# Forming all MLP weight sums on VectorE, and handing the residual stream between two layers through HBM

## The chip, the cores and the metric

One NeuronCore of a Trainium2 chip runs the whole program. The metric is the device time of one execution in microseconds (us). Inputs and weights lie in HBM; the output is written back to HBM. TensorE is called PE in the views, VectorE DVE, ScalarE ACT, GpSimd POOL, and SyncE SP.

## What is computed

The program carries a residual stream x of 1024 frames by 1024 features through two layers, in float32. Layer 0 mixes frames by a gated linear recurrence, layer 1 by an attention with forget gates (FoX, 8 heads); beside either one runs an attention into 256 fixed memory tokens. Each layer then adds a squared-ReLU MLP:

```
for layer in range(2):
    h = rms_norm(x, norm_mix[layer])
    y_mix, xq = rglru_group(h, ...) if layer == 0 else fox_group(h, ...)
    y_mem = memory_group(xq, mem, norm_mem[layer], w_mem_kv[layer], ...)
    x = x + concatenate([y_mix, y_mem]) @ w_out[layer]
    x = x + square(relu(rms_norm(x, norm_mlp[layer]) @ w_mlp_in[layer])) @ w_mlp_out[layer]
```

## The kernel before

**Products.** Each float32 operand is split into a high part, which TensorE takes in its faster float32 form, and a low part, the remainder; a product is three matmuls (high by high, high by low, low by high). The high part of a weight is a copy on ScalarE (L316), the low part a subtraction (L317, on VectorE, for some entries half of it on GpSimd). Activations are split the same way: L468 and L469 in `split`, L474 and L477 in `split_sb`. SP loads raw weights into four buffers `wr`; the split parts go through a ring of three pairs `wh`, `wl`. The list `plan` fixes in which order the weights come.

**Stream.** x is kept transposed, as 8 blocks of 128 features, in two halves of 512 frames, h=0 and h=1. Between stages it lies in HBM, in `xspill` (`self.xs`). `load_x` (L510) brings one block of 128x512 into one of the `f` tiles; `r` tiles hold split activations.

**MLP.** Each layer's MLP runs in 8 groups of hidden features, and each group as two block products of Strassen's kind (`mlp_z`, then `mlp_out`), with seven products of sums of blocks instead of eight of blocks. One product (L1017) is 24 matmuls of 128x512. The seven weight operands of a block product are a unit: the raw blocks a11, a12, a21, a22 and the sums S1 to S4, which `_wunit` forms in place when it reaches S2 (L355 to L357, in two halves of 512, and L360). Only the first unit of a layer's `w1` forms them on VectorE, the others on GpSimd. Some groups of layer 1 are parked: their first two products run earlier, in other stages, so that their unit begins with S2.

In `mlp_out` the block results c11, c21, c22 and c12 leave PSUM as a copy on ScalarE (L1028) and a sum on VectorE (L1033). In groups 0 to 6 a result is then added in HBM by an accumulating DMA of GpSimd (`send`, L1172). In group 7 of both layers the old x is added on the chip instead: for c11 by GpSimd (L1192) from tiles loaded before, for c21 and c22 by an accumulating DMA from HBM into the tile (L1195), for c12 by starting from a loaded tile. Then `sink` stores the block by SP (L1177). In layer 0 `sink` also squares each block on ScalarE (L438), sums the squares (L444, on GpSimd, a few on VectorE) and, for the half h=0, splits it as the input of layer 1's mixer.

**After layer 0.** `kv` projects the memory tokens (L385; its norm's products are L590, the sum of its squares L597 on GpSimd). `norm_fin` turns the sum of squares into the norm factor: four one-column matmuls (L378) add over the partitions. `xq_proj` projects the memory queries of h=0, `fox_proj` queries, keys and values, `fox` is the attention, `outproj` the output projection, run once for the attention's half of the weights (`wout1x`) and once for the memory's (`wout1m`), each in 8 pieces with a weight entry of 512 columns apiece. `weave(a, b, rate)` runs steps of b between steps of a.

The program's text is put into each engine's order by a scheduler at compile time; every engine then works through its own list, with semaphores between them.

## Time and profile before

| | us |
|---|---|
| median of three runs | 2134.29 |
| lowest and highest of the runs | 2131.2 and 2135.48 |
| the profiled execution | 2132.37 |
| its span in the trace | 2130.7 |
| TensorE busy in it | 2071.5 |
| VectorE busy | 1663.3 |
| ScalarE busy | 1141.9 |
| GpSimd busy | 864.0 |

1.7 us of the profiled execution lie outside its span. Layer 0's MLP lies from about 340 to 985 us of the span, layer 1's from about 1530 to the end; the handover between the layers is the stretch from about 930 to 1005 us.

How to read the rows: in a timeline, start, duration, engine, line, operation, output<-input with the tile shape, and a count; in brackets the idle time of the engine before it and what ended it. In a group of instructions: the count, then busy time, the mean in ns, and idle time. In a list of waits: total, times, longest. L12 is line 12 of the kernel.

### The profile page before, as it was taken

Reading aid. Unit: us, or ns where it says so; the run is one execution under the profiler, and the core shown is the slowest. Engines: PE = TensorE matmul, PEld = TensorE weight load, DVE = VectorE, ACT = ScalarE, POOL = GpSimd, SP = SyncE. Lnnn points to the kernel's source line nnn. Section 1 sums busy time; section 2 is a strip of 40 time slices with the busy share of each in tenths; the row PEclk is TensorE's granted clock in tenths of the full one; section 3 lists DMA queues with packets and bytes.
Section 4 is the critical chain, followed back from the end, with each engine's and each line's share of the span. In section 5 each row is a group of like instructions: output and inputs, shape, how many; then the busy total and the mean of one; then the engine's idle time right before and its main releaser. Section 6 shows DMA issues by size and latency. Waiting matters only on the chain. (4 is left out here: it accounts for less than half of the span.)

```text
span 2130.7 us, 30055 instructions
## 1 busy us (share of the span) xinstructions
PE 2071.5 (97%) x10466; PEld 1727.4 (81%) x10466; DVE 1663.3 (78%) x2708; ACT 1141.9 (54%) x2160; POOL 864.0 (41%) x844
## 2 busy tenths in 40 slices
PE   9999999999999999988999999999999999999998
PEld 8898878878778778767998998777777877787786
DVE  7988698877877877887677778776787768868777
ACT  6755655544454454555555646566544554445443
POOL 2222321535535525545342333422054645445444
PEclk8999999999999999989999999999999999999999
DMA  5422452546545635627768446934546675364474
GB/s 180 140 77 93 135 184 94 101 89 128 101 97 119 111 87 119 156 86 199 276 218 290 133 138 214 299 122 129 161 99 139 138 150 101 85 140 94 89 173 119
DMA packets 126392, 298.44 MB, mean 140 GB/s; under 512 B 14176, under 2 KB 16288, under 8 KB 126240
## 3 DMA queue, kind: packets, MB, share of 16 engines
q1 hardware_dynamic: 82464, 208.36, 29.4%
q0 software_dynamic: 43776, 88.17, 23.2%
q8 instruction: 82, 1.34, 0.3%
q14 instruction: 70, 0.57, 0.1%
HBM read 187.32 MB, written 109.15 MB: 139 GB/s over the span
## 5 line engine op out<-in xcount | busy, mean ns | idle before, releaser
L317 DVE TENSOR_TENSOR wl<-wr,wh 128x1024 fp32r<-128x1024 f32 (+2 forms) x362 | 441.2, 1229 | 108.5 <-ACT wh L316 104.1
L1017 PE MATMUL pspt<-r,wh 128*128 128x512 f32 x1536 | 485.1, 396 | 7.2 <-DVE r L477 2.6
L1172 POOL DMA_DIRECT2D xspill<-f x224 | 284.7, 1963 | 287.5 <-DVE f L1033 284.1
L316 ACT ACTIVATE wh<-wr 128x1024 fp32r<-128x1024 f32 (+3 forms) x411 | 306.0, 766 | 141.4 <-PE pss L1017 41.2
L1017 PEld LDWEIGHTS pspt<-r,wh 128*128 128x128 f32 x1536 | 289.0, 188 | 77.9 <-DVE r L477 4.3
L1017 PE MATMUL pss<-r,wh 128*128 128x512 f32 x1024 | 329.6, 400 | 19.8 <-ACT f L1028 8.1
L477 DVE TENSOR_TENSOR r<-f,r 128x512 fp32r<-128x512 f32 x282 | 230.1, 826 | 98.5 <-ACT r L474 39.9
L1017 PE MATMUL pspt<-r,wl 128*128 128x512 f32 x768 | 305.6, 398 | 0.2
L1017 PE MATMUL pspj<-r,wh 128*128 128x512 f32 x832 | 265.8, 399 | 2.1 <-DVE f L1033 1.0
L1017 PEld LDWEIGHTS pss<-r,wh 128*128 128x128 f32 x1024 | 192.6, 189 | 75.9 <-DVE r L477 13.9
L385 PE MATMUL pspj<-wh,r 128*128 128x256 f32 (+1 forms) x1280 | 248.5, 286 | 2.3 <-DVE r L1322 0.8
L474 ACT ACTIVATE r<-f 128x512 fp32r<-128x512 f32 x282 | 173.5, 626 | 106.2 <-DMA xspill<-f 49.0
L1038 ACT ACTIVATE f<-f 128x512 f32<-128x512 f32 x128 | 80.9, 632 | 269.5 <-DVE f L1037 269.4
L385 PEld LDWEIGHTS pspj<-wh,r 128*128 128x128 f32 x1280 | 201.6, 188 | 5.3 <-DVE r L1322 1.0
L1017 PE MATMUL pss<-r,wl 128*128 128x512 f32 x512 | 203.6, 398 | 0.0
L355 POOL TENSOR_TENSOR wr<-wr,wr 128x512 f32<-128x512 f32 x60 | 95.7, 1778 | 249.0 <-DVE wl L317 233.2
L1017 PEld LDWEIGHTS pspj<-r,wh 128*128 128x128 f32 x832 | 156.3, 189 | 39.4 <-DVE r L469 1.5
L385 PE MATMUL pspj<-wl,r 128*128 128x256 f32 (+1 forms) x640 | 181.1, 283 | 0.0
L1017 PEld LDWEIGHTS pspt<-r,wl 128*128 128x128 f32 x768 | 146.0, 190 | 36.9 <-DVE wl L317 2.0
L385 PE MATMUL pspj<-r,wh 128*128 128x512 f32 x488 | 164.1, 411 | 5.3 <-ACT r L474 2.1
L1017 PE MATMUL pspj<-r,wl 128*128 128x512 f32 x416 | 163.4, 397 | 0.6 <-DVE wl L317 0.5
L357 POOL TENSOR_TENSOR wr<-wr,f 128x512 f32<-128x512 f32 x60 | 135.4, 2550 | 17.1 <-issue 17.1
(301 smaller groups left out, 4035.3 us busy)
## 6 DMA issues: line engine op xcount, KB each, us to landing
wr<-in_w_dram SPq DMA_DIRECT2D x136, 512.0 KB, 4.5
xspill<-f POOLq DMA_DIRECT2D x224, 256.0 KB, 7.0
f<-xspill SPq DMA_DIRECT2D x88, 256.0 KB, 4.1
xspill<-f SPq DMA_DIRECT2D x64, 256.0 KB, 3.5
f<-in_xT_dram SPq DMA_DIRECT2D x32, 256.0 KB, 3.5
wr<-in_wkv_dram SPq DMA_DIRECT2D x16, 512.0 KB, 3.6
...
```

The source lines that it names most:

```text
L316: self.wact = self.nc.scalar.activation(hi, raw, AF.Copy)
L317: eng.tensor_tensor(lo, raw, hi.bitcast(F32), ALU.subtract)
L355: G.tensor_tensor(r["a11"][:, d], r["a11"][:, d], r["a21"][:, d], ALU.subtract)
L357: G.tensor_tensor(r["a12"][:, d], r["a12"][:, d], x, ALU.subtract)
L385: self.lastmm = self.nc.tensor.matmul(out, lhsT=a, rhs=b, start=(j == 0), stop=(j == n - 1))
L474: i = self.nc.scalar.activation(hi[:, :n], src, AF.Copy)
L477: self.nc.vector.tensor_tensor(lo[:, :n], src, hi[:, :n].bitcast(F32), ALU.subtract)
L1017: self.lastmm = self.nc.tensor.matmul(ps, lhsT=a, rhs=b, start=(start and c == 0 and j == 0), stop=(c == n - 1 and j == 2), skip_group_che ...
L1038: self.lastsq = self.nc.scalar.activation(f[:, n], f[:, n], AF.Square)
L1172: nc.gpsimd.dma_start(self.xs[2 * q + a, :, b * H:(b + 1) * H], f[:, n], accum_op=ALU.add)
```

## The change

Four things are edited. Every weight unit of the MLP forms its sums on VectorE (`u.dve = True`). Group 7 of layer 0 now does what groups 0 to 6 do: it adds its results in HBM by accumulating DMAs of GpSimd. The next mixer's half h=0 is then loaded from HBM, in the order of blocks 0, 2, 4, 6, 1, 3, 5, 7, by a new `norm_split_back`, which splits each block, squares it on ScalarE and adds over the partitions on TensorE (`sq_pe`: four one-column matmuls for each of the 8 blocks). It is woven one step for one into the memory projection. The squares of h=1 are taken where `norm_split` loads that half, during the fox projection. In layer 1's last group, the c11 add moves from GpSimd to VectorE and behind the second sum. And the entries of `wout1m` and `wout1x` hold two pieces each, 1024 columns wide.

```diff
@@ -463,9 +463,11 @@
                                       start=(m == 0 and t == 0), stop=(m == 7), skip_group_check=True)
             self.F.put(sq)
 
-    def split(self, xt, g, n=H):
+    def split(self, xt, g, n=H, behind=None):
         hi, lo = self.R.get(), self.R.get()
         self.last_hi = self.nc.scalar.activation(hi[:, :n], xt, AF.Copy, scale=g)
+        if behind is not None:
+            self.after(self.last_hi, behind)
         self.nc.vector.scalar_tensor_tensor(lo[:, :n], xt, g, hi[:, :n].bitcast(F32), ALU.mult, ALU.subtract)
         return hi, lo
 
@@ -517,6 +519,15 @@
             if stats:
                 self.sqacc(k, h, x[:, :H])
             xs.append(self.split(x[:, :H], self.pc(g, k)))
+            self.F.put(x)
+            yield
+
+    def norm_split_back(self, h, g, src):
+        xs = self.xg[h] = [None] * 8
+        for j, k in enumerate((0, 2, 4, 6, 1, 3, 5, 7)):
+            x = self.load_x(k, h, src)
+            xs[k] = self.split(x[:, :H], self.pc(g, k), behind=self.wact)
+            self.sq_pe(j, h, x[:, :H], self.last_hi)
             self.F.put(x)
             yield
 
@@ -888,12 +899,15 @@
 
     def outproj(self, h, ks, src, dst, gain, last, banks=("pj",)):
         nc = self.nc
+        per = 8 // len(ks)
         for m in range(8):
             x = self.load_x(m, h, src)
-            wh, wl = self.wnext()
+            if m % per == 0:
+                wh, wl = self.wnext()
             ps = self.psum(banks[m % len(banks)])
             terms = []
             for i, k in enumerate(ks):
+                i += m % per * len(ks)
                 c = slice(i * P, (i + 1) * P)
                 terms += self.t3(wh[:, c], wl[:, c], *(self.ymix[h][k] if k < 4 else self.ymem[h][k - 4]))
             yield from self.mmq(ps, terms, 6)
@@ -1004,8 +1018,9 @@
             self.plan_unit("w1", 8 * l + g, Unit.ALL[1:2])
         for g in range(8):
             u = self.plan_unit("w1", 8 * l + g, Unit.ALL[2:] if g in parked + wait else Unit.ALL)
-            u.dve = g == 0
-            self.plan_unit("w2", 8 * l + g)
+            u.dve = True
+            u = self.plan_unit("w2", 8 * l + g)
+            u.dve = True
 
     def product(self, banks, parts, start, done=None):
         w = self.wnext()
@@ -1152,10 +1167,9 @@
 
     def mlp_out(self, l, g, mid):
         nc = self.nc
-        V, G = nc.vector, nc.gpsimd
+        V = nc.vector
         n = slice(0, H)
         hp = self.hp
-        seen = set()
 
         def run(banks, key, start, done, ahead=None):
             if ahead is not None:
@@ -1172,14 +1186,10 @@
             nc.gpsimd.dma_start(self.xs[2 * q + a, :, b * H:(b + 1) * H], f[:, n], accum_op=ALU.add)
             self.F.put(f)
 
+        last = l == 1 and g == 7
+
         def sink(f, q, a, b):
-            x, dm = f[:, n], 2 * q + a
-            nc.sync.dma_start((self.out if l else self.xs)[dm, :, b * H:(b + 1) * H], x)
-            if l == 0:
-                self.sqacc(1 if b in seen else 0, b, x, V if b == 0 and a == 1 else None)
-                seen.add(b)
-                if b == 0:
-                    self.xg[0][dm] = self.split(x, self.pc("gmix1", dm))
+            nc.sync.dma_start(self.out[2 * q + a, :, b * H:(b + 1) * H], f[:, n])
             self.F.put(f)
 
         def keep(a, b):
@@ -1187,21 +1197,21 @@
 
             def first(q, ps):
                 self.copies(dst)(q, ps)
-                if g == 7 and a == b == 0:
-                    f = self.acc.pop(0)
-                    G.tensor_tensor(dst[q][:, n], dst[q][:, n], f[:, n], ALU.add)
-                    self.F.put(f)
-                elif g == 7:
+                if last and (a or b):
                     nc.gpsimd.dma_start(dst[q][:, n], self.xs[2 * q + a, :, b * H:(b + 1) * H], accum_op=ALU.add)
 
             def then(q, ps):
                 self.plus(dst[q], ps)
-                (sink if g == 7 else send)(dst[q], q, a, b)
+                if last and not (a or b):
+                    f = self.acc.pop(0)
+                    V.tensor_tensor(dst[q][:, n], dst[q][:, n], f[:, n], ALU.add)
+                    self.F.put(f)
+                (sink if last else send)(dst[q], q, a, b)
 
             return first, then
 
         def end(q, ps):
-            if g == 7:
+            if last:
                 self.plus(acc[q], ps)
                 sink(acc[q], q, 0, 1)
             else:
@@ -1217,7 +1227,7 @@
         mid()
         yield from run(A, "t2", False, c21[0], "t1")
         C = [self.psum(k) for k in more]
-        acc = [self.load_x(2 * q, 1, self.xs) for q in range(4)] if g == 7 else None
+        acc = [self.load_x(2 * q, 1, self.xs) for q in range(4)] if last else None
         yield from run(C, "t3", True, c22[0], "t4")
         yield from run(A, "t1", False, c22[1], "b22")
         yield from run(C, "t4", False, c21[1])
@@ -1236,7 +1246,7 @@
         def hook7(key):
             if key in ("t2", "b22") and nxt is not None:
                 advance(nxt)
-            if key == "t1":
+            if key == "t1" and l:
                 self.acc = [self.load_x(2 * q, 0, self.xs) for q in range(4)]
 
         for p in wait:
@@ -1252,7 +1262,6 @@
                 self.F.put(*self.rsb)
                 if l == 0:
                     self.pool_parts = TUNE["pb0"]
-                    self.xg[0] = [None] * 8
             drain(self.mlp_out(l, g, lambda: self.mlp_back(g + 1)))
 
 
@@ -1531,17 +1540,17 @@
         self.plan_mv("wxqb")
         self.plan_fox(0)
         self.plan_fox(1)
-        self.plan += [self.ent("wout1m", m, 512, 1) for m in range(8)]
+        self.plan += [self.ent("wout1m", m, 1024, 1) for m in range(4)]
         self.plan_mv("wxqb")
         self.plan_fox(0)
         self.plan_fox(1)
-        self.plan += [self.ent("wout1x", m, 512, 1) for m in range(8)]
-        self.plan += [self.ent("wout1m", m, 512, 1) for m in range(8)]
+        self.plan += [self.ent("wout1x", m, 1024, 1) for m in range(4)]
+        self.plan += [self.ent("wout1m", m, 1024, 1) for m in range(4)]
         for g in TUNE["park"]:
             self.plan_unit("w1", 8 + g, Unit.ALL[:2])
         for g in TUNE["wait"]:
             self.plan_unit("w1", 8 + g, Unit.ALL[:1])
-        self.plan += [self.ent("wout1x", m, 512, 1) for m in range(8)]
+        self.plan += [self.ent("wout1x", m, 1024, 1) for m in range(4)]
         self.plan_mlp(1, TUNE["park"], TUNE["wait"])
 
         self.share()
@@ -1635,19 +1644,21 @@
 
 
         self.fox_setup()
-        advance(kv, 5)
+        advance(kv, 6)
+        weave(kv, self.norm_split_back(0, "gmix1", self.xs), 1.0)
+        self.vst = {}
+        xq = self.xq_proj(0, 1)
+        advance(xq, 4)
         self.norm_fin(0, False, self.lastmm)
-        drain(kv)
-        self.vst = {}
-        drain(self.xq_proj(0, 1))
-        self.norm_fin(1, False)
+        drain(xq)
         xa = self.xattn(0)
         self.pool_parts = TUNE["pb0"]
         weave(self.fox_proj(0, 0), xa, TUNE["fp00"])
         drain(xa)
         fx = self.fox(0)
         opm = self.outproj(0, K_M, self.xs, self.xs, None, False)
-        weave(self.fox_proj(0, 1), self.norm_split(1, "gmix1", self.xs, False), 0.5)
+        weave(self.fox_proj(0, 1), self.norm_split(1, "gmix1", self.xs, True), 0.5)
+        self.norm_fin(1, False)
         self.xg_free(0)
 
         def second():
@@ -1730,6 +1741,8 @@
     kord = [4, 5, 6, 7, 0, 1, 2, 3]
     for nme, w, ks in (("wout0", w0, kord), ("wout1m", w1, kord[0:4]), ("wout1x", w1, kord[4:8])):
         o[nme] = st(C(w[ks].reshape(-1, D)))
+        if len(ks) == 4:
+            o[nme] = C(o[nme].reshape(4, 2, P, 512).transpose(0, 2, 1, 3).reshape(4, P, 1024))
     w1, w2 = [], []
     for l in range(2):
         w = f["w_mlp_in"][l].reshape(4, 2, P, 8, 2, 2, P).transpose(3, 5, 1, 2, 4, 0, 6).reshape(8, 4, P, 1024)

```

The engines' order in the compiled programs, as rows of line, operation, output<-input, shape and the semaphores waited for. In a tile's name, `f_856_8078` is use 856 of the `f` tiles, while the number of `wr`, `wh` and `wl` is a buffer's; `xspill` is x in HBM. First GpSimd at the end of layer 0's last group. Before:

```order
L597 TENSOR_TENSOR f_838_7994<-f_838_7994,f_849_8026 128x512 [waits Activation_49,Pool_49]
L1192 TENSOR_TENSOR f_860_8102<-f_860_8102,f_830_7911 128x512 [waits DMAHW0_49,Activation_49]
L1192 TENSOR_TENSOR f_861_8111<-f_861_8111,f_831_7913 128x512 [waits DMAHW1_49,Activation_49]
L1192 TENSOR_TENSOR f_862_8120<-f_862_8120,f_832_7915 128x512 [waits DMAHW2_49,Activation_49]
L1192 TENSOR_TENSOR f_863_8129<-f_863_8129,f_833_7917 128x512 [waits DMAHW3_49,Activation_49]
L444 TENSOR_TENSOR f_868_8154<-f_868_8154,f_871_8168 128x512 [waits PE_49,Activation_49]
L444 TENSOR_TENSOR f_868_8154<-f_868_8154,f_874_8183 128x512 [waits Activation_49,Pool_49]
L1269 MEMSET f_924_8492 128x128 [waits PE_49]
L1270 AFFINE_SELECT f_924_8492<-f_924_8492 128x128 [waits Pool_49]
L444 TENSOR_TENSOR f_868_8154<-f_868_8154,f_877_8198 128x512 [waits Activation_49]
L1195 DMA f_884_8221<-xspill 128x512 [waits DMASW0_49,Activation_49]
L1195 DMA f_885_8230<-xspill 128x512 [waits DMASW1_49,Activation_49]
```

After:

```order
L608 TENSOR_TENSOR f_834_7970<-f_834_7970,f_845_8002 128x512 [waits Activation_49,Pool_49]
L1186 DMA xspill<-f_856_8078 128x512 [waits DMASW0_49,DVE_49]
L1186 DMA xspill<-f_857_8086 128x512 [waits DMASW1_49,DVE_49]
L1186 DMA xspill<-f_858_8094 128x512 [waits DMASW2_49,DVE_49]
L1186 DMA xspill<-f_859_8102 128x512 [waits DVE_49]
L1186 DMA xspill<-f_876_8213 128x512 [waits DMASW4_49,DVE_49]
L317 TENSOR_TENSOR wl_76<-wr_69,wh_73 128x256 [waits DMAHW4_49,PE_49,Activation_49]
L1186 DMA xspill<-f_877_8221 128x512 [waits DMASW5_49,DVE_49]
L1186 DMA xspill<-f_878_8229 128x512 [waits DMASW6_49,DVE_49]
L317 TENSOR_TENSOR wl_76<-wr_69,wh_73 128x256 [waits PE_49,Activation_49]
L1186 DMA xspill<-f_879_8237 128x512 [waits DMASW7_49,DVE_49]
L1186 DMA xspill<-f_868_8166 128x512 [waits DMASW0_49,DVE_49]
```

The adds of c11 (L1192), the sums of squares (L444) and the accumulating loads (L1195) are gone; the sends (L1186: c11's `f_856` to `f_859`, c22's `f_876` to `f_879`, then c21's from `f_868`) stand there, with the halves of the memory weights' splits (L317) between them.

Next SP's list at the same place, from the last loads of x before the stores. Before:

```order
L510 DMA f_889_8257<-xspill 128x512 [waits DMAHW0_49,DMASW5_49,PE_49]
L510 DMA f_888_8255<-xspill 128x512 [waits DMAHW1_49,DMASW4_49,PE_49]
L510 DMA f_890_8259<-xspill 128x512 [waits DMAHW2_49,DMASW6_49,PE_49]
L510 DMA f_891_8261<-xspill 128x512 [waits DMAHW3_49,DMASW7_49]
L1177 DMA xspill<-f_860_8102 128x512 [waits DMAHW4_49,DVE_49]
L312 DMA wr_69<-in_wkv_dram 128x1024 [waits DMAHW5_49,DVE_49,Pool_49]
L1177 DMA xspill<-f_861_8111 128x512 [waits DMAHW6_49,DVE_49]
L1177 DMA xspill<-f_862_8120 128x512 [waits DMAHW7_49,DVE_49]
L1177 DMA xspill<-f_863_8129 128x512 [waits DMAHW0_49,DVE_49]
L312 DMA wr_71<-in_wkv_dram 128x1024 [waits DMAHW1_49,DVE_49,Pool_49]
```

After, some steps later, among the weights of the query projection (`wxqb`):

```order
L312 DMA wr_69<-in_wxqb_dram 128x1024 [waits DMAHW1_49,DMAHW5_49,DVE_49,Pool_49]
L512 DMA f_899_8542<-xspill 128x512 [waits DMASW1_49,DVE_49,Activation_49]
L312 DMA wr_70<-in_wxqb_dram 128x1024 [waits DMAHW2_49,DVE_49,Pool_49]
L512 DMA f_907_8624<-xspill 128x512 [waits DMASW2_49,DMAHW6_49,DVE_49,Activation_49]
L312 DMA wr_71<-in_wxqb_dram 128x1024 [waits DMAHW3_49,Pool_49]
L512 DMA f_911_8650<-xspill 128x512 [waits DMASW3_49,PE_49]
L512 DMA f_915_8675<-xspill 128x512 [waits DMASW0_49,PE_49]
L512 DMA f_919_8701<-xspill 128x512 [waits DMASW1_49,DMAHW4_49,PE_49,Activation_49]
L312 DMA wr_72<-in_wxqb_dram 128x1024 [waits DMAHW5_49,DVE_49,Pool_49]
L512 DMA f_923_8746<-xspill 128x512 [waits DMASW2_49,PE_49]
```

The stores (L1177) are replaced by loads of x (L512) that wait for an accumulating DMA (DMASW) to have landed; weight loads stand behind them in the list.

Last, VectorE in a group of layer 1 whose unit begins with S2. Before, the sums of that unit are on GpSimd:

```order
L477 TENSOR_TENSOR r_1778_16425<-f_1729_16083,r_1777_16424 128x512 [waits DVE_49]
L317 TENSOR_TENSOR wl_76<-wr_72,wh_73 128x1024 [waits DMAHW4_49,PE_49,Activation_49]
L477 TENSOR_TENSOR r_1780_16429<-f_1730_16097,r_1779_16428 128x512 [waits Activation_49]
L317 TENSOR_TENSOR wl_77<-wr_70,wh_74 128x1024 [waits PE_49,Activation_49]
L1033 TENSOR_TENSOR f_1773_16398<-f_1773_16398,pss_16232 128x512 [waits PE_49]
L1033 TENSOR_TENSOR f_1774_16406<-f_1774_16406,pss_16233 128x512 [waits PE_49]
L317 TENSOR_TENSOR wl_78<-f_1781_16469,wh_75 128x512 [waits Activation_49]
L1033 TENSOR_TENSOR f_1775_16414<-f_1775_16414,pspj_16234 128x512 [waits DMASW6_49,PE_49]
L1033 TENSOR_TENSOR f_1776_16422<-f_1776_16422,pspj_16235 128x512 [waits PE_49]
L317 TENSOR_TENSOR wl_78<-f_1782_16475,wh_75 128x512 [waits Activation_49]
```

After:

```order
L355 TENSOR_TENSOR wr_69<-wr_69,wr_71 128x512 [waits DMAHW3_49,DMAHW2_49]
L355 TENSOR_TENSOR wr_69<-wr_69,wr_71 128x512
L479 TENSOR_TENSOR r_1776_16327<-f_1732_16005,r_1775_16326 128x512 [waits Activation_49]
L356 TENSOR_TENSOR f_1785_16410<-wr_72,wr_69 128x512 [waits DMAHW4_49,DVE_49,PE_49]
L356 TENSOR_TENSOR f_1786_16416<-wr_72,wr_69 128x512 [waits DVE_49]
L360 TENSOR_TENSOR wr_71<-wr_71,wr_72 128x1024
L479 TENSOR_TENSOR r_1782_16366<-f_1733_16024,r_1781_16365 128x512 [waits DVE_49]
L479 TENSOR_TENSOR r_1784_16370<-f_1734_16038,r_1783_16369 128x512 [waits Activation_49]
L1048 TENSOR_TENSOR f_1779_16355<-f_1779_16355,pspj_16175 128x512 [waits DMASW4_49,DMASW3_49,PE_49]
L317 TENSOR_TENSOR wl_76<-wr_70,wh_73 128x1024 [waits Activation_49]
L1048 TENSOR_TENSOR f_1780_16363<-f_1780_16363,pspj_16176 128x512 [waits PE_49,Activation_49]
L317 TENSOR_TENSOR wl_77<-f_1786_16416,wh_74 128x512 [waits Activation_49]
```

The sums (L355, L356, L360, and L357 a little below) stand among the splits of activations (L477 before, L479 now), the low halves (L317) and the sums from PSUM (L1033 before, L1048 now). The first two wait for the raw weights' loads (DMAHW).

## The prediction

> **What bounds the kernel now.** I read the page's busy shares first, then TensorE's (PE's) waits, then the stretches where it waits, engine by engine.
>
> ```profile
> span 2130.7 us, 30055 instructions
> PE 2071.5 (97%) x10466; PEld 1727.4 (81%) x10466; DVE 1663.3 (78%) x2708; ACT 1141.9 (54%) x2160; POOL 864.0 (41%) x844
> ```
>
> TensorE is busy for 2071.5 of 2130.7 us, so the change can win only what TensorE idles, 59 us in all, and what it runs at a lowered clock. Taking work off GpSimd (POOL), or adding some to VectorE (DVE), is worth nothing by itself. The question is which of the 59 us lie where the change acts. Busy times by stretch come next: the columns are PE, PEld, DVE, ACT, POOL, then the granted clock, DMA share and GB/s. The first stretch is one whole MLP group in the middle of layer 0, the others lie where layer 0 ends and layer 1 begins.
>
> ```profile
> 553.50:632.30 78.80, 78.43 (x336) 62.69 (x335) 60.01 (x64) 37.48 (x61) 36.97 (x30) 1.00 0.52 106
> ...
> 938.50:943.10 4.60, 2.02 (x9) 1.32 (x9) 4.60 (x6) 3.40 (x6) 3.90 (x4) 1.00 0.00 0
> 943.10:957.00 13.90, 8.85 (x20) 5.43 (x21) 13.90 (x19) 8.40 (x14) 4.42 (x4) 0.54 0.25 82
> ...
> 997.50:1004.00 6.50, 5.83 (x28) 5.62 (x29) 6.39 (x15) 2.73 (x8) 5.15 (x6) 0.61 0.61 206
> ```
>
> In a middle group TensorE idles 0.37 of 78.80 us: nothing is to be had there. Between the layers it idles, and where it has idled its granted clock falls to 0.54 and 0.61. The waits of TensorE from 900 to 1005 us (total, times, longest) say on whom:
>
> ```profile
> PE pspt L385 <- DVE wl L317: 3.7, 2, 2.6
> PE pspt L1017 <- DVE r L477: 2.6, 1, 2.6
> PE pss L1017 <- ACT r L474: 2.2, 1, 2.2
> PE pspt L1017 <- DVE f L1033: 2.1, 1, 2.1
> PE pss L1017 <- DVE r L477: 1.7, 2, 1.3
> PE pspt L1017 <- DVE f L1037: 1.1, 1, 1.1
> PE pss L1017 <- DVE f L1033: 1.1, 1, 1.1
> PE pspj L1017 <- DVE f L1033: 1.0, 1, 1.0
> ```
>
> These sum to 15.5 us. Nearly all are waits for VectorE, which is busy without a break from 938.5 to 957. Its own rows show why, and GpSimd's beside them:
>
> ```profile
> 932.23 5.52 DVE L590 SCALAR_TENSOR_TENSOR r<-f,par,r 128x256 fp32r<-128x256 f32 x4
> ...
> 941.30 1.75 DVE L477 TENSOR_TENSOR r<-f,r 128x512 fp32r<-128x512 f32 x1
> ...
> 946.94 0.68 DVE L477 TENSOR_TENSOR r<-f,r 128x512 fp32r<-128x512 f32 x1
> ...
> 979.67 0.69 DVE L1033 TENSOR_TENSOR f<-f,pss 128x512 f32<-128x512 f32 x1 [6.66 <-DMA f<-xspill]
> ```
>
> ```profile
> 934.54 4.33 POOL L597 TENSOR_TENSOR f<-f,f 128x512 f32<-128x512 f32 x3
> ...
> 939.58 6.29 POOL L1192 TENSOR_TENSOR f<-f,f 128x512 f32<-128x512 f32 x4 [0.70 <-ACT f L1028]
> ...
> 966.04 7.07 POOL L1195 DMA_DIRECT2D f<-xspill  x8 [2.47 <-ACT f L1028]
> ```
>
> The same VectorE split (L477) takes 1.75 us while GpSimd adds (L1192) and 0.68 us when GpSimd is quiet. So GpSimd's elementwise work costs VectorE about 1.07 us an instruction here, VectorE falls behind, and TensorE waits. Later VectorE stands 6.66 us for the accumulating load that GpSimd issued at 966.04.
>
> **The change part by part.** *The end of layer 0* loses the L1192 adds, the L1195 loads with VectorE's wait for them, the squares' sums and VectorE's next-mixer splits out of the last MLP group; the group ends like the others, which lose 0.37 us. Recoverable are the 15.5 us of waits and the low clock: 8.85 x (1 - 0.54) = 4.1 and 5.83 x (1 - 0.61) = 2.3, together 21.9 us. [...]
>
> Not all of it comes back. The 3.7 us of waits for the low halves of the memory weights (L317) stay in my sum: half of these splits now stand in GpSimd's queue between the new accumulating sends. Between 0 and 3.7 + 2.3 (its clock), I take 3.7. New on TensorE are the statistics of half the columns: 32 one-column matmuls for 4. The nearest row has 8 of them:
>
> ```profile
> 1488.07 1.05 PE L462 MATMUL pso<-cD,f 128*128 128x1 f32 x8 [0.52 <-ACT f L449]
> ...
> 991.05 0.40 PE L385 MATMUL pspt<-wh,r 128*128 128x256 f32 x2
> ...
> 994.93 0.40 PE L385 MATMUL pspt<-wh,r 128*128 128x256 f32 x2
> ```
>
> That is 0.13 us each, in a stretch that I take to be at low clock; so 28 more cost between 1.8 (half of that) and 3.7 us, and I take 2.8, the middle. This end is therefore worth 21.9 - 3.7 - 2.8 = 15.4 us.
>
> That holds if the reload of x is hidden. The new chain is: last column sums on VectorE, accumulating send, load by SP, split, next projection. Sends and loads take (issue to landing, min/median/max; the first line is L1172's, the second L510's):
>
> ```profile
> DMA to landing us min/median/max: 3.8/7.0/16.1
> DMA to landing us min/median/max: 2.5/3.9/8.5
> ```
>
> The c21 blocks, the last that this half needs, are summed one product (24 matmuls, 5.6 us at the 0.233 us that 336 matmuls in 78.43 us give) before the group's last matmul, T0. With 1.6 us for sum and issue they land at T0 - 4 + 7.0 = T0 + 3, are loaded by T0 + 7, and four splits of 0.7 us on ScalarE and VectorE bring them to about T0 + 10. TensorE has the memory projection first: 33 matmuls of 256 columns from 991.05 to 994.93, 0.118 us each, so 8 pieces of 24 end at T0 + 23, plus the statistics. That is a cover of 13 us; SP's weight loads that now stand behind the x loads share it. The rest of the change there (16 stores on SP become sends on GpSimd, the squares stay on ScalarE) lies on engines that TensorE doesn't then wait for. The second half's squares and sums move into the fox projection, where they are to be done by the end of some 24 products: I cost them at nothing, up to 2 us if GpSimd's seven sums are late.
>
> *The weight sums on VectorE.* Its own durations, from the units that it already forms, and what its weight split costs in the middle group against alone:
>
> ```profile
> L356 DVE TENSOR_TENSOR f<-wr,wr 128x512 f32<-128x512 f32 x4 | 2.7, 680 | 0.5 <-DMA wr<-in_w_dram 0.5
> L357 DVE TENSOR_TENSOR wr<-wr,f 128x512 f32<-128x512 f32 x4 | 2.7, 676 | 0.0
> L355 DVE TENSOR_TENSOR wr<-wr,wr 128x512 f32<-128x512 f32 x4 | 2.6, 684 | 1.2 <-DMA wr<-in_w_dram 1.2
> L360 DVE TENSOR_TENSOR wr<-wr,wr 128x1024 f32<-128x1024 f32 x2 | 2.4, 1212 | 0.0
> ...
> L317 DVE TENSOR_TENSOR wl<-wr,wh 128x1024 fp32r<-128x1024 f32 x12 | 20.9, 1743 | 5.6 <-ACT wh L316 5.6
> ...
> 920.55 1.22 DVE L317 TENSOR_TENSOR wl<-wr,wh 128x1024 fp32r<-128x1024 f32 x1
> ```
>
> One unit is 2 x 0.680 + 2 x 0.676 + 2 x 0.684 + 1.212 = 5.3 us, two units a group 10.6 us. VectorE goes from 60.0 to at most 70.6 of 78.8 us, and gets back 12 x (1.743 - 1.22) = 6.3 us on these splits alone, as GpSimd no longer sums beside it. It does not become the bound: 0 us, and at best TensorE's idle 0.37 us in 14 groups, 5 us.
>
> *The parked groups of layer 1* are where it can hurt. There the sums wait for raw weights (waits between 1530 and 1780 us; then VectorE's own idling near the second such wait):
>
> ```profile
> PE pss L1017 <- ACT f L1028: 8.1, 3, 3.9
> POOL wr L355 <- DMA wr<-in_w_dram: 15.7, 3, 7.3
> POOL f L356 <- DMA wr<-in_w_dram: 8.1, 2, 5.6
> ```
>
> ```profile
> 1646.09 0.69 DVE L477 TENSOR_TENSOR r<-f,r 128x512 fp32r<-128x512 f32 x1 [1.29 <-DMA xspill<-f]
> 1650.32 1.42 DVE L477 TENSOR_TENSOR r<-f,r 128x512 fp32r<-128x512 f32 x2 [3.54 <-ACT r L474]
> ```
>
> GpSimd waits 23.8 us for raw weights, in two or three places of some 10 us. On VectorE such a wait holds up what is queued behind: the splits of the activations (L477), the low halves (L317) and the PSUM sums (L1033), for all of which TensorE waits. VectorE idles there anyway, 1.29 + 3.54 = 4.8 of about 10 us, so some 5 us in each of two groups are new. Below nothing: the 8.1 us of TensorE's waits for ScalarE (its copies stand behind a split whose buffer still waits for a send to land) could go, as GpSimd sends sooner. Bounds -8.1 and +23.8; I take +3, a third of the 10 new ones, since the queues between VectorE and TensorE held back about as much at the median of such waits: TensorE's 8.1 us beside GpSimd's 23.8.
>
> *The last group of layer 1* loses GpSimd's sums beside VectorE and its own c11 adds:
>
> ```profile
> PE pss L1017 <- DVE r L477: 3.1, 1, 3.1
> ...
> L477 DVE TENSOR_TENSOR r<-f,r 128x512 fp32r<-128x512 f32 x8 | 11.5, 1454 | 0.0
> ...
> 2090.01 5.09 POOL L1192 TENSOR_TENSOR f<-f,f 128x512 f32<-128x512 f32 x3 [2.98 <-ACT f L1028]
> ```
>
> VectorE lost 8 x (1.454 - 0.68) = 6.2 us on splits there; TensorE's 3.1 us wait goes, with about 1 us of low clock behind it, against four adds of 0.68 us that come later: -4, bounds -5 and 0. *Output weights in pairs* are the same bytes in half the entries, and the order around them changes (all eight pieces of the memory part now stand ahead of the first fox head): 0, bounds -3 and +3 from waits of 1 to 3 us such as those above.
>
> Sum: -15.4 + 0 + 3 - 4 + 0 = -16.4 us. Against the profiled execution (2132.4 us, 1.7 of it outside the span) that is 2116.0; the median of the runs, 2134.3, lies 1.9 above it, so I say 2117.5.
>
> **The rivals.** *Stalls in layer 1 go too*: with GpSimd free, sends land sooner, and ScalarE's buffer waits vanish: -8.1 in place of +3, 2106. For it: those sends were queued among sums. Against: the first gap (1562 to 1567 us) has VectorE late, too.
>
> *VectorE stands in line for raw weights* (the slower side). If all 23.8 us reach TensorE in five waits, and each is followed by a low clock as in the row at 0.54 (about 2 us each), that is 33.8 instead of 3: 2148. It decides from 21 us on, that is when over 85% of GpSimd's waits pass on to TensorE. For it: VectorE works in order, as its 6.66 us stand shows; against: its own idling at those places, and that loads start sooner when sums take 5.3 us. [...]
>
> *The reload is late*: sends landing at the longest 16.1 and loads at 8.5 us make T0 - 4 + 16.1 + 8.5 + 3 = T0 + 24, where the cover ends; with SP's queue behind, 8 us of stall and clock: 2126. The median of 7.0 speaks against it.
>
> *The gain moves on*: the transition only changes which engine is late (sends before splits on GpSimd, SP's loads), and all but the tail is given back: about 2132, no change.
>
> **How the numbers follow.** Forecast, 2108 to 2124: 0.57. Stalls in layer 1 go: 0.13. Late reload: 0.12. No gain: 0.09. VectorE stands: 0.09. A measurement can tell 0.2%, 4.3 us, from no change. Faster takes the first three, 0.82; same 0.09, slower 0.09. The range leaves out the slow case and the last of the no-change case at the top, and little below the second at the bottom: 2104 to 2131.
>
> **What would show it.** Right: TensorE's waits between the layers fall from 15.5 to about 4 us at clock 1.0; VectorE's L477 is near 0.68 us and its 1024-wide L317 near 1.22; a middle group still takes 78.8 us; no wait for the x load ahead of the query projection. Wrong: VectorE's waits for the raw weight loads in layer 1 followed by TensorE waits of the same length, a middle group longer than 79 us, or TensorE waiting behind GpSimd's L317 or for the reload.

## The result, and the profile after

| | before | after |
|---|---|---|
| median, us | 2132.74 (4 runs) | 2115.76 (4 runs) |
| lowest and highest | 2130.55 to 2135.48 | 2110.05 to 2117.22 |
| ratio, 95% interval | 1 | 0.9911 (0.989 to 0.9933) |
| profiled execution, its span | 2132.37, 2130.7 | 2116.66, 2113.8 |

The changed kernel is 0.9% faster. Lines have moved: L477 is now L479, L1017 is L1032, L1028 and L1033 are L1043 and L1048, the sends L1172 are L1186, the memory norm's L590 and L597 are L601 and L608. The page of the kernel after begins:

```profile
span 2113.8 us, 29923 instructions
...
PE 2069.8 (98%) x10522; PEld 1738.4 (82%) x10522; DVE 1576.6 (75%) x2906; ACT 1156.2 (55%) x2156; POOL 493.3 (23%) x615
```

GpSimd's busy time fell from 864.0 to 493.3 us. VectorE, which took its sums over, did not become busier: 1663.3 before, 1576.6 now. TensorE works as long as before (2071.5, now 2069.8); its idle time went from 59.2 to 44.0 us, and that is 15.2 of the 16.9 us by which the span is shorter. The same middle group as in the prediction, and then the stretch in which TensorE was last slowed at layer 0's end (the columns are busy time and count of PE, PEld, DVE, ACT and POOL, then clock, DMA share and GB/s):

```profile
553.50:632.30 78.80, 78.80 (x341) 63.72 (x340) 56.35 (x80) 39.43 (x61) 14.34 (x18) 1.00 0.51 108
942.30:947.00 4.70, 4.66 (x14) 3.69 (x14) 4.70 (x8) 2.02 (x4) 0.67 (x2) 0.64 0.37 107
```

TensorE no longer idles at all in the middle group. VectorE executes 80 instructions there instead of 64 in less time (56.35 for 60.01 us). TensorE's largest waits from 900 to 1015 us, which answer to the list of 15.5 us before:

```profile
PE pspt L1032 <- DVE r L479: 3.6, 1, 3.6
PE pso L462 <- ACT f L449: 1.2, 2, 0.7
PE pspj L385 <- ACT r L468: 0.4, 1, 0.4
```

One wait of size is left, 3.6 us, and the clock of 0.64 above lies right behind it. To see where the 17 us came from I set marks on the same matmuls in both traces, the matmuls of one kernel line counted along TensorE's list, and took the difference of the times at which they end:

| mark (its time before, us) | after minus before, us |
|---|---|
| A: in layer 0's last MLP group (899.5) | -1.2 |
| B: end of layer 0's MLP (987.9) | -13.1 |
| C: layer 1's projections begun, statistics done (1076.3) | -12.2 |
| D: end of the attention stage (1472.0) | -6.2 |
| E: layer 1's MLP begun (1528.6) | -3.4 |
| F: past the parked groups (1776.0) | -9.6 |
| G: in layer 1's last group (2089.5) | -12.1 |
| H: last matmul (2126.9) | -18.1 |

Some 11 us are won from A to C. From C to E 9 are lost again, which the prediction didn't have. From E to H 15 are won, more than it had.

### The profile page after: what moved, and what is told of

Read it like the earlier page. It is cut to its first block, busy times and chain, and to the rows that moved or that the text cites. A ratio compares the mean times of both kernels' runs of the same rounds, so it can differ in the third digit from the quotient of the medians.

```text
span 2113.8 us, 29923 instructions
## 1 busy us (share of the span) xinstructions
PE 2069.8 (98%) x10522; PEld 1738.4 (82%) x10522; DVE 1576.6 (75%) x2906; ACT 1156.2 (55%) x2156; POOL 493.3 (23%) x615
## 5 line engine op out<-in xcount | busy, mean ns | idle before, releaser
L1032 PE MATMUL pspt<-r,wh 128*128 128x512 f32 x1536 | 491.8, 396 | 8.8 <-DVE f L1048 3.9
L317 DVE TENSOR_TENSOR wl<-wr,wh 128x1024 fp32r<-128x1024 f32 (+2 forms) x354 | 346.0, 987 | 195.2 <-ACT wh L316 193.6
L1186 POOL DMA_DIRECT2D xspill<-f x240 | 210.7, 1058 | 848.5 <-DVE f L1048 816.7
L1032 PEld LDWEIGHTS pspt<-r,wh 128*128 128x128 f32 x1536 | 288.4, 188 | 78.3 <-DVE r L479 4.6
L1032 PE MATMUL pss<-r,wh 128*128 128x512 f32 x1024 | 327.6, 395 | 1.3 <-DVE r L479 1.1
L1032 PE MATMUL pspt<-r,wl 128*128 128x512 f32 x768 | 304.9, 397 | 0.0
L1032 PE MATMUL pspj<-r,wh 128*128 128x512 f32 x832 | 271.9, 400 | 2.3 <-DVE f L915 2.1
L479 DVE TENSOR_TENSOR r<-f,r 128x512 fp32r<-128x512 f32 x282 | 190.8, 694 | 73.7 <-DMA xspill<-f 51.4
L1032 PEld LDWEIGHTS pss<-r,wh 128*128 128x128 f32 x1024 | 192.5, 188 | 47.2 <-DVE r L479 2.0
L476 ACT ACTIVATE r<-f 128x512 fp32r<-128x512 f32 x282 | 169.2, 625 | 71.5 <-DMA xspill<-f 21.1
L1032 PE MATMUL pss<-r,wl 128*128 128x512 f32 x512 | 202.4, 396 | 0.0
L1032 PEld LDWEIGHTS pspj<-r,wh 128*128 128x128 f32 x832 | 156.8, 190 | 40.0 <-DVE f L915 2.6
L1032 PEld LDWEIGHTS pspt<-r,wl 128*128 128x128 f32 x768 | 146.2, 190 | 35.4
L385 PE MATMUL pspj<-r,wh 128*128 128x512 f32 x488 | 163.0, 410 | 5.7 <-DMA wh<-wsp 2.1
L1032 PE MATMUL pspj<-r,wl 128*128 128x512 f32 x416 | 165.6, 399 | 0.0
L385 PEld LDWEIGHTS pspj<-wl,r 128*128 128x128 f32 x640 | 121.3, 190 | 0.7 <-issue 0.2
L1032 PEld LDWEIGHTS pss<-r,wl 128*128 128x128 f32 x512 | 97.0, 190 | 23.5
```

The lines of the kernel that those rows point to most:

```text
L317: eng.tensor_tensor(lo, raw, hi.bitcast(F32), ALU.subtract)
L385: self.lastmm = self.nc.tensor.matmul(out, lhsT=a, rhs=b, start=(j == 0), stop=(j == n - 1))
L476: i = self.nc.scalar.activation(hi[:, :n], src, AF.Copy)
L479: self.nc.vector.tensor_tensor(lo[:, :n], src, hi[:, :n].bitcast(F32), ALU.subtract)
L1032: self.lastmm = self.nc.tensor.matmul(ps, lhsT=a, rhs=b, start=(start and c == 0 and j == 0), stop=(c == n - 1 and j == 2), skip_group_che ...
L1186: nc.gpsimd.dma_start(self.xs[2 * q + a, :, b * H:(b + 1) * H], f[:, n], accum_op=ALU.add)
```

## The experiments

Four parts were tried alone or left out: the weight sums, the handover through HBM, the pairs of output weights, and the c11 add of layer 1's last group (in `handover_only` and in all that keep the handover it is included). Then single costs were taken away or moved. This table has the marks of all of them, each trace against the trace of before. One execution's stage can be off by about 4 us: `c11_add` has before's order of instructions in everything but the last group, and its marks still drift by up to 3.5 us. So I read only what is larger, or what comes back in several kernels.

| kernel | A | B | C | D | E | F | G | H |
|---|---|---|---|---|---|---|---|---|
| the whole change | -1.2 | -13.1 | -12.2 | -6.2 | -3.4 | -9.6 | -12.1 | -18.1 |
| sums_only | -2.3 | -3.2 | -3.6 | -4.5 | -4.8 | -10.4 | -12.9 | -12.6 |
| handover_only | +1.6 | -6.9 | -3.8 | +4.4 | +2.5 | +8.4 | +8.3 | +4.0 |
| pairs_only | -1.1 | -1.5 | -2.8 | -5.0 | -2.3 | +0.5 | +0.2 | +0.2 |
| sums_and_handover | -3.4 | -15.3 | -14.1 | -8.0 | -7.9 | -14.0 | -16.4 | -22.3 |
| sums_and_handover_2 | -3.3 | -15.2 | -14.5 | -10.1 | -8.8 | -12.4 | -14.2 | -20.1 |
| c11_add | +0.6 | +0.5 | +0.6 | -0.6 | +1.6 | +3.5 | +3.4 | -1.0 |
| stats_on_vector | -4.6 | -16.6 | +0.7 | +5.2 | +5.8 | +2.2 | -0.1 | -6.0 |
| kv_squares_vector | -3.2 | -17.4 | -13.4 | -5.4 | -4.8 | -13.2 | -15.2 | -21.1 |
| both_on_vector | -2.2 | -16.5 | +0.4 | +4.3 | +4.6 | -2.6 | -4.0 | -9.9 |
| parked_on_gpsimd | -3.5 | -15.5 | -14.7 | -7.5 | -5.4 | -10.7 | -12.8 | -18.7 |
| no_second_statistics | -0.9 | -12.8 | -10.1 | -11.3 | -8.2 | -16.2 | -18.3 | -24.3 |
| early_statistics | -4.1 | -18.3 | -4.7 | -5.1 | -5.2 | -11.6 | -14.1 | -20.0 |

**The weight sums alone.** The kernel before, with

```
-            u.dve = g == 0
-            self.plan_unit("w2", 8 * l + g)
+            u.dve = True
+            u = self.plan_unit("w2", 8 * l + g)
+            u.dve = True
```

> The kernel before with one edit: all weight sums of the MLP on VectorE. Theory 1 (GpSimd's elementwise work holds up VectorE): layer 1's MLP gains what it gained with the whole change, about 14 us from its start to the end (parked groups 6, middle groups 3, last group 4 to 6), and the last group of layer 0 some 3 to 5 us more, so 2114 to 2118 us. Rival (the gain in layer 1 comes from the handover, since the order of the whole program was newly laid out): no more than 5 us, 2128 or above.

Measured: 2118.07 us against 2133.62, ratio 0.993 (0.9914 to 0.9946). TensorE's waits from 900 to 1005 us, and what GpSimd does there:

```profile
PE pspt L1018 <- DVE r L477: 7.8, 1, 7.8
PE pspt L385 <- DVE wl L317: 3.7, 2, 2.5
PE pss L1018 <- DVE r L477: 3.4, 1, 3.4
PE pspj L1018 <- DVE f L1034: 1.1, 1, 1.1
```

```profile
932.23 4.67 POOL L597 TENSOR_TENSOR f<-f,f 128x512 f32<-128x512 f32 x3 [34.83 <-ACT f L593]
936.86 5.67 POOL L1193 TENSOR_TENSOR f<-f,f 128x512 f32<-128x512 f32 x4
```

With the weight sums gone, GpSimd stood idle for 34.83 us before these adds, and still they lie side by side with VectorE's work: the waits sum to 16.0 us, as many as before (15.5). So at the end of layer 0 it is not enough to take the sums off GpSimd; alone, their move wins about 1 us from A to C. It wins most in layer 1, 5.6 us from E to F and 7.8 from E to H, where I had expected 14.

**The handover alone.** The changed kernel, with the two flags above set back and single output weights:

> The changed kernel with the weight sums back on GpSimd and the output weights back in single pieces: only the handover between the layers (and the c11 add of the last group on VectorE) differs from before. Theory 1: the stretch between the layers gains 9 to 12 us, layer 1's MLP nothing, 2121 to 2124 us, and if the losses of the attention stage belong to the handover, 2127 to 2130. Rival: the handover gives nothing without the sums on VectorE, since GpSimd must then send and sum in the same group: 2131 or above.

Measured: 2134.38 against 2133.62, ratio 1.0011 (0.9998 to 1.0023): nothing. It wins 5.4 us from A to C, loses 8.2 from C to D and 5.9 from E to F, and wins 4.3 in the last group. Its waits from 900 to 1015 us:

```profile
PE pspt L1028 <- ACT r L476: 4.1, 1, 4.1
PE pspt L1028 <- DVE f L1048: 2.0, 1, 2.0
PE pso L462 <- ACT f L449: 1.3, 2, 1.0
```

**The pairs alone.** The kernel before, with the output weights' entries 1024 wide:

```
-        self.plan += [self.ent("wout1m", m, 512, 1) for m in range(8)]
+        self.plan += [self.ent("wout1m", m, 1024, 1) for m in range(4)]
```

and the same for `wout1x`, with the steps of `outproj` and the host's layout as in the change.

> The kernel before with one edit: the output weights of layer 1 in pairs. Theory 1: the 6 to 8 us that TensorE lost in the attention stage (1250 to 1400 us) come from the pairs, whose earlier and larger weight entries change the order there: 2138 to 2141 us. Rival: the pairs cost nothing, and the loss comes from the second half's squares and the later start of the first half: 2131 to 2135.

Measured: 2140.11 (10 runs) against 2133.62, ratio 1.0035 (1.0021 to 1.0048): slower. The execution that was profiled was the fastest of the ten (2133.73 us), and its marks stay within 5 us of before, so this trace doesn't show where the time goes in the others.

**Sums and handover, without the pairs.** The changed kernel with single output weights, measured twice:

> The changed kernel with the output weights back in single pieces. Theory 1 (the pairs cost 6 to 8 us in the attention stage): 2108 to 2110 us. Rival (the loss there belongs to the handover): 2114 to 2117, as the whole change.

> The handover and the sums on VectorE with output weights in single pieces, once more beside the other two, as their base. Every theory: 2111 to 2115 us; were it 2116 or more, the single pieces would not be better than the pairs of the whole change (2115.8).

Measured: 2113.03, ratio 0.9909 (0.9892 to 0.9927), and 2112.28, ratio 0.9898 (0.9881 to 0.9915). The whole change has 0.9911, so within it the pairs can't be told from nothing. From A to C the two together win 10.7 and 11.2 us, where the parts alone won 1.3 and 5.4: they need each other.

**The c11 add alone.** The kernel before, where only layer 1's last group adds the old x to c11 on VectorE, behind the second sum:

```
+                    if l == 0:
+                        f = self.acc.pop(0)
+                        G.tensor_tensor(dst[q][:, n], dst[q][:, n], f[:, n], ALU.add)
+                        self.F.put(f)
...
+                if l and g == 7 and not (a or b):
+                    f = self.acc.pop(0)
+                    V.tensor_tensor(dst[q][:, n], dst[q][:, n], f[:, n], ALU.add)
+                    self.F.put(f)
```

> The kernel before with one edit: the c11 add of layer 1's last group on VectorE, behind the second sum. Theory 1 (GpSimd's four adds hold up VectorE there, and the profile of the sums alone still shows TensorE's 3.35 us wait in that group): the last group gains 5 to 6 us, 2127 to 2129 us. Rival (the gain of the last group needs both, the adds and the weight sums off GpSimd): at most 2 us, 2131 or above.

Measured: 2131.32 against 2133.73, ratio 0.9983 (0.9973 to 0.9993). The total lies where the rival had it (2131 or above); the last group comes near what theory 1 has (5 to 6 us), as it wins 4.4 us from G to H. TensorE's only wait from 2060 us to the end, first in this kernel, then in `sums_only` (a timeline row, its wait in brackets):

```profile
PE pss L1017 <- ACT r L474: 0.7, 1, 0.7
```

```profile
2084.41 0.80 PE L1018 MATMUL pss<-r,wh 128*128 128x512 f32 x1 [3.35 <-DVE r L477]
```

The 3.1 us wait of before goes with the four adds, while GpSimd still forms its weight sums; without the weight sums but with the adds it stays. Every kernel that has the moved add wins from G to H: 4.3 and 4.4 us where GpSimd still forms the weight sums, 5.9 to 6.0 in the nine where it doesn't. The two without the moved add win nothing there.

**The first half's statistics on VectorE.** Sums and handover, where the squares of the reloaded blocks are added by VectorE and only four one-column matmuls follow:

```
-            self.sq_pe(j, h, x[:, :H], self.last_hi)
+            self.sqacc(j, h, x[:, :H], self.nc.vector, self.last_hi)
```

> The handover and the sums on VectorE, output weights in single pieces (2113 us before this edit), with the squares of the reloaded half added up by VectorE, so that 4 one-column matmuls follow and not 32. Theory 1 (each of these is two instructions of about 0.1 us on TensorE, 5.7 us for the 28): 2107 to 2109 us, no gap at the reload. Rival (TensorE's time there is hidden by waits for the reload, or VectorE comes late with seven more adds of 0.7 us): 2112 to 2115.

Measured: 2127.78, ratio 0.9967 (0.9955 to 0.9979), some 15 us slower than with the statistics on TensorE. TensorE's largest wait from 960 to 1030 us, SP's largest there, and its row for three of the loads of x; then the same row in `sums_and_handover`:

```profile
PE pspj L385 <- ACT r L468: 10.7, 4, 5.5
...
SPq L512 <- DVE f L444: 24.8, 6, 7.9
```

```profile
1006.09 13.68 SPq L512 DMA_DIRECT2D f<-xspill  x3
```

```profile
989.64 3.92 SPq L512 DMA_DIRECT2D f<-xspill  x3
```

This is the late reload of the prediction's rivals. The loads (L512) wait for VectorE's adds (L444), since the tile that a load needs is free only when an earlier square has been added. So load, split, square, add and the next load follow one another, and SP's loads spread over 13.68 us instead of 3.92. VectorE isn't busy meanwhile: from 1000 to 1010 us it works 5.68 us, from 1010 to 1020 us 2.71. The marks lose 17.3 us from B to C.

**The memory norm's squares on VectorE.** Sums and handover, with layer 1's three adds of L608 on VectorE:

```
-                nc.gpsimd.tensor_tensor(ss[:, :H], ss[:, :H], sq[:, :H], ALU.add)
+                (nc.vector if l else nc.gpsimd).tensor_tensor(ss[:, :H], ss[:, :H], sq[:, :H], ALU.add)
```

> The handover and the sums on VectorE, output weights in single pieces (2113 us before this edit), with the three adds of the memory tokens' squares in layer 0's last group on VectorE too, so that GpSimd does no elementwise work there. Theory 1 (VectorE's three steps that took 4.4 us were held up by GpSimd's adds, and the one wait left there, 3.65 us, goes with its low clock): 2108 to 2110 us. Rival (VectorE has too much to do at this place, with or without GpSimd): the wait stays between 2.5 and 4 us, 2112 to 2115.

Measured: 2109.06, ratio 0.988 (0.9863 to 0.9896). The kernel after has these adds on GpSimd. First TensorE's wait there, then VectorE's three products and GpSimd's three adds, each by itself, and then VectorE's row of the same three products in `kv_squares_vector`:

```profile
942.34 0.79 PE L1032 MATMUL pspt<-r,wh 128*128 128x512 f32 x1 [3.64 <-DVE r L479]
...
936.33 1.52 DVE L601 SCALAR_TENSOR_TENSOR r<-f,par,r 128x256 fp32r<-128x256 f32 x1
937.78 1.51 DVE L601 SCALAR_TENSOR_TENSOR r<-f,par,r 128x256 fp32r<-128x256 f32 x1
939.21 1.48 DVE L601 SCALAR_TENSOR_TENSOR r<-f,par,r 128x256 fp32r<-128x256 f32 x1
...
934.36 3.21 POOL L608 TENSOR_TENSOR f<-f,f 128x512 f32<-128x512 f32 x1 [10.76 <-ACT f L604]
937.65 1.35 POOL L608 TENSOR_TENSOR f<-f,f 128x512 f32<-128x512 f32 x1
939.08 1.33 POOL L608 TENSOR_TENSOR f<-f,f 128x512 f32<-128x512 f32 x1
```

```profile
934.96 1.27 DVE L601 SCALAR_TENSOR_TENSOR r<-f,par,r 128x256 fp32r<-128x256 f32 x3
```

The three products take 4.36 us beside GpSimd and 1.27 without it, and TensorE's wait of 3.6 us becomes one of 1.8. The adds end at 937.57, 939.00 and 940.41 us, the products at 937.85, 939.29 and 940.69: each product ends 0.3 us behind an add.

The total is the lowest of the versions that keep the computation, but its interval meets those of `sums_and_handover`, so the 3 to 4 us are not established in the total.

**Both of these edits together.** Sums and handover with the two edits above:

> Both edits together: the reloaded half's squares and the memory tokens' squares are added on VectorE. Theory 1: the gains add up, 2102 to 2105 us. Rival: VectorE becomes late in one of the two places, 2107 or above.

Measured: 2125.29, ratio 0.9962 (0.9951 to 0.9974). From B to C it loses 16.9 us, as `stats_on_vector` does: the late reload again, and less work of GpSimd's beside VectorE doesn't mend it.

**The parked groups' sums back on GpSimd.** Sums and handover, where the four first units of layer 1 that begin late (at S1 or S2) are again formed by GpSimd:

```
-            u.dve = True
+            u.dve = not (l == 1 and g in parked + wait)
```

> The handover and the sums on VectorE, output weights in single pieces (2113 us before this edit), with the sums of the first weight units of layer 1's parked groups (four of 32 units) back on GpSimd. Theory 1 (the gain of 5 to 6 us there comes from these units: on GpSimd each takes 13 us and holds up both VectorE's splits and the sends behind it): 2117 to 2120 us, with TensorE's waits between 1530 and 1780 us back at 6 to 8 us. Rival of my forecast (VectorE's standing in line for raw weights costs, and GpSimd is the better place for these four units): 2108 to 2111 us. Rival 2 (the gain there comes from the other units): 2112 to 2114.

Measured: 2115.34, ratio 0.9909 (0.9892 to 0.9926); `sums_and_handover_2`, on the same chip, 2112.28: not to be told apart. The waits for raw weights from 1530 to 1780 us, on GpSimd in this kernel:

```profile
POOL wr L355 <- DMA wr<-in_w_dram: 17.4, 3, 6.8
POOL f L356 <- DMA wr<-in_w_dram: 7.8, 2, 5.1
```

and on VectorE in the kernel after, with TensorE's there:

```profile
DVE f L356 <- DMA wr<-in_w_dram: 2.6, 2, 1.4
DVE wr L357 <- DMA wr<-in_w_dram: 1.0, 2, 0.6
DVE wr L355 <- DMA wr<-in_w_dram: 0.8, 1, 0.8
...
PE pspt L1032 <- DVE f L1048: 3.6, 2, 3.1
PE pss L1032 <- DVE r L479: 1.1, 1, 1.1
```

GpSimd waits 25.2 us for what VectorE waits 4.4 us. From E to F this kernel wins 5.3 us and the whole change 6.2.

**The second half's statistics left out.** Sums and handover, where the second half takes over the first half's norm factor, and its squares and sums are not formed:

```
-        weave(self.fox_proj(0, 1), self.norm_split(1, "gmix1", self.xs, True), 0.5)
-        self.norm_fin(1, False)
+        weave(self.fox_proj(0, 1), self.norm_split(1, "gmix1", self.xs, False), 0.5)
+        self.vx[1], self.rs_tok[1] = self.vx[0], self.rs_tok[0]
```

> The handover and the sums on VectorE, output weights in single pieces (2113 us before this edit), with the statistics of the second half left out: no squares, sums and norm factor for h=1, the factor of h=0 is used in its place (so the result of half the frames is not the reference's). Theory 1 (these 8 squares on ScalarE, 7 sums on GpSimd and the norm factor on VectorE stand ahead of the first attention head's preparation, and cost the 5 to 7 us that the attention stage lost): 2106 to 2109 us. Rival (the stage's loss comes from the shifted start of the first half, and the statistics are hidden): 2111 to 2114.

Measured: 2104.41, ratio 0.9864 (0.9848 to 0.9881), against 2112.28 for `sums_and_handover_2` on the same chip: these statistics cost 7.9 us, give or take 5 by the two intervals. From C to D this kernel wins 1.2 us where the kernels that take these statistics in the fox projection lose 3.9 to 8.2. The fox projection and the first part of the attention (busy time and count by engine, as above), in this kernel and then in `sums_and_handover`:

```profile
1080.00:1140.00 60.00, 58.99 (x419) 54.40 (x419) 46.18 (x131) 29.99 (x66) 14.02 (x18) 1.00 0.78 272
1140.00:1300.00 160.00, 157.53 (x1220) 151.16 (x1219) 119.88 (x368) 92.15 (x235) 56.65 (x93) 1.00 0.49 159
```

```profile
1080.00:1140.00 60.00, 58.34 (x402) 53.36 (x401) 49.35 (x132) 28.61 (x60) 18.94 (x20) 1.00 0.82 287
1140.00:1300.00 160.00, 154.78 (x1207) 148.32 (x1206) 116.72 (x368) 91.30 (x235) 54.87 (x94) 1.00 0.46 151
```

During the fox projection, where these statistics are taken, TensorE idles 1.0 us without them and 1.7 with them; in the attention behind it 2.5 and 5.2 (4.9 in `sums_and_handover_2`). So most of what they cost comes up behind the stage that they stand in.

**The second half's statistics early.** `kv_squares_vector`, with the second half loaded once more, squared and summed during the memory query projection, ahead of the fox projection:

```
+        def stat1():
+            for k in range(8):
+                x = self.load_x(k, 1, self.xs)
+                self.sqacc(k, 1, x[:, :H])
+                self.F.put(x)
+                yield
+            self.norm_fin(1, False)
...
+        weave(xq, st1, 0.5)
```

> The handover, the sums and the memory tokens' squares on VectorE, output weights in single pieces (2109 us before this edit), with the second half's statistics taken earlier: its 8 blocks are loaded once more during the memory query projection, squared and summed there, and not ahead of the first attention head. Theory 1 (it is the place that costs: there the 8 squares and 7 sums stand ahead of the head's preparation, earlier ScalarE has room): 2101 to 2105 us. Rival (they cost some 7 us wherever they stand, or the eight more loads of 256 KB hold up the weights in SP's queue): 2108 to 2114.

Measured: 2113.58, ratio 0.9894 (0.9878 to 0.9911): no gain over 0.988. The loss from C to D is gone (it wins 0.4), but from B to C 13.6 us are lost, where `kv_squares_vector` loses 4.0. There, the statistics of one block on TensorE and a split of the first half on ScalarE, with their waits, and the window around them:

```profile
997.97 1.05 PE L462 MATMUL pso<-cD,f 128*128 128x1 f32 x8 [1.85 <-ACT f L449]
...
996.68 0.72 ACT L468 ACTIVATE r<-f,par 128x512 fp32r<-128x512 f32 x1 [1.97 <-DMA f<-xspill]
```

```profile
995.00:1015.00 20.00, 17.48 (x95) 17.06 (x94) 13.29 (x23) 12.89 (x30) 7.44 (x8) 0.66 0.73 244
```

ScalarE stands 1.97 us for a load of the first half, in a stretch in which SP now has eight more loads to issue; TensorE waits 1.85 us for the square behind it, and its clock falls to a mean of 0.66 over 20 us. What was saved from C to D is lost between the layers.

## Why the prediction was right in the total, point by point

The total is as forecast, 2116.66 us for the profiled execution against a sum of 2116.0, and 0.9911 against 2117.5 / 2134.3 = 0.992. But it is right by errors that cancel: that they cancel is luck. (The sum and its 1.9 us make 2117.9; I wrote 2117.5.)

| term | forecast | measured in the trace after |
|---|---|---|
| end of layer 0 (A to C) | -15.4 | -11.0 |
| attention and output projection (C to E), the second statistics and the pairs | 0 | +8.8 |
| parked groups (E to F) | +3 | -6.2 |
| middle groups of layer 1 (F to G) | 0, at best some us | -2.5 |
| last group (G to H) | -4 | -6.0 |
| ahead of A, and behind the last matmul | 0 | -1.2 + 1.2 |
| sum | -16.4 | -16.9 |

*The end of layer 0.* The mechanism was right: elementwise work of GpSimd made VectorE late, and that made TensorE wait and run slow (before, 13.3 of its 15.5 us of waits were for VectorE, at clocks of 0.54 and 0.61). The row for it is the middle group's low halves (L317), in the kernel after:

```profile
L317 DVE TENSOR_TENSOR wl<-wr,wh 128x1024 fp32r<-128x1024 f32 x13 | 15.9, 1224 | 12.1 <-ACT wh L316 12.1
```

1224 ns for 1743 before, as forecast. Beside GpSimd's adds VectorE's instructions took longer: a split 1.75 us, and 0.68 without them; the three products shown above 4.36, and 1.27 without them. Not all of VectorE's work took longer. Over the whole kernel before, its splits of tiles in SBUF (L477) and its sums with one input from PSUM (L1033) took, in ns (least, median, most):

```profile
L477 DVE TENSOR_TENSOR r<-f,r x282: 670/682/2885, 20.6 to 2105.0; 128x512 fp32r<-128x512 f32 x141
L1033 DVE TENSOR_TENSOR f<-f,pspt x128: 669/677/691, 363.1 to 2123.1; 128x512 f32<-128x512 f32 x128
```

44 of these 128 sums ran for 0.45 us or more beside a sum of GpSimd's, and none of the 44 took longer than 0.68 us.

Three sizes were off. I let all waits on VectorE go, but the memory norm's adds stayed on GpSimd: 3.6 us of wait and 4.66 x (1 - 0.64) = 1.7 of low clock are left. I kept 3.7 us for the waits on L317, which went. And the statistics cost double: I took the row at 1488.07 us to be at low clock, where it was 1.00, and read its "x8" as eight matmuls. It is four, as each of these float32 matmuls with one column leaves two records:

```profile
988.30 0.95 PE L462 MATMUL pso<-cD,f 128*128 128x1 f32 x8
989.11 0.36 PE L385 MATMUL pspt<-wh,r 128*128 128x256 f32 x1
```

One block takes 989.11 - 988.30 = 0.81 us at full clock (1.00 in these 0.81 us), so 28 matmuls more are 7 x 0.81 = 5.7 us, not 2.8. With these sizes the forecast would be 15.4 - 3.6 - 1.7 + 3.7 - 2.9 = 10.9 us, against 11.0 measured. Even so the statistics are better there than as sums on VectorE (`stats_on_vector`).

*The parts don't add up.* I treated the sums as worth nothing by themselves at layer 0's end and the handover as the whole of it. Alone the handover gives 5.4 us there and nothing in the total (1.0011); with the sums off GpSimd, 10.7. Sums, handover and pairs measured alone would add up to 0.993 - 1 + 1.0011 - 1 + 1.0035 - 1 = -0.24%; together they give -0.89%. Without the pairs it is -0.59% apart, and -0.91% and -1.02% together.

*The reload hidden.* Right: TensorE waits 0.4 us for it (L468). Sends and loads landed in about the times I had used (7.0 and 4.3 us at the median):

```profile
xspill<-f POOLq DMA_DIRECT2D x240, 256.0 KB, 7.0
f<-xspill SPq DMA_DIRECT2D x88, 256.0 KB, 4.3
```

But the cover is thinner than my 13 us say, since the loads also need free tiles: `stats_on_vector` turned that into 10.7 us of waits.

*The second half's statistics.* This is the step that failed: "I cost them at nothing, up to 2 us". They cost 7.9 us (`no_second_statistics`). I priced them in the fox projection, and there they do cost little; what I left out is what stands behind them, the attention, where TensorE idles 2.7 us more. From 1080 to 1135 us ScalarE's squares wait for the loads of x in `sums_and_handover`; without the squares the splits (L468) wait for the same loads, but less:

```profile
ACT f L438 <- DMA f<-xspill: 9.0, 4, 3.0
```

```profile
ACT r L468 <- DMA f<-xspill: 4.2, 4, 2.3
```

That ScalarE holds up the attention's first heads by this is argued and not shown: whether its squares, GpSimd's sums or the norm factor decide was not separated, and the idle times above account for some 3 of the 8 us.

*VectorE not the bound.* Right: 56.35 of 78.80 us. What I overlooked is how slow GpSimd was at the sums. Its groups in the middle group of the kernel before:

```profile
L357 POOL TENSOR_TENSOR wr<-wr,f 128x512 f32<-128x512 f32 x4 | 10.6, 3079 | 1.2 <-issue 1.2
L356 POOL TENSOR_TENSOR f<-wr,wr 128x512 f32<-128x512 f32 x4 | 9.0, 2772 | 0.0
L360 POOL TENSOR_TENSOR wr<-wr,wr 128x1024 f32<-128x1024 f32 x2 | 7.4, 3696 | 0.0
L355 POOL TENSOR_TENSOR wr<-wr,wr 128x512 f32<-128x512 f32 x4 | 6.4, 1848 | 16.9 <-DVE wl L317 16.9
```

Two units were 10.6 + 9.0 + 7.4 + 6.4 = 33.4 us of GpSimd's, 16.7 each, against 5.3 on VectorE. An add of 128x512 didn't always take GpSimd as long: of the three shown above the first took 3.21 us, the others 1.35 and 1.33. By 16.7 and 5.3 us I estimate that on VectorE a unit can be ready up to 11 us sooner, and its raw buffers free.

*The parked groups.* Forecast +3, measured -6.2, a wrong sign. I assumed that a wait of GpSimd's for raw weights would become a wait of about that length on VectorE. It waits 4.4 us for them, GpSimd 23.8, and TensorE's waits there fell from 8.5 to 4.7 us. That these four units moved is not what wins most: with them back on GpSimd the stage still wins 5.3 us. What remains is that the other units left GpSimd: `sums_only` wins 5.6 us there without the handover, `handover_only` loses 5.9 without the sums. Whether it is by earlier sends, as one of my rivals had it, or by buffers that come free earlier, was not separated.

*The last group.* The size is right within 2 us, and the 3.1 us wait went (TensorE has none there from 2040 us to the end), but I had counted GpSimd's weight sums as a cause beside its c11 adds. The c11 adds alone give 4.4 us (`c11_add`) and the weight sums alone nothing (`sums_only`); both together give 5.9 to 6.0.

*The pairs.* Forecast 0 with bounds of 3. Alone they are slower, by 0.35%, about 7 us, with a cause that stays open; in the whole change their part is below what can be told.

*The rivals.* "Stalls in layer 1 go too" was the better guess for layer 1, and the late reload exists but did not come in. VectorE stood only 4.4 us in line for raw weights.
